# Low parts of weights by an adding DMA, expert picks by head, 40 U blocks ahead: a decoder block on one NeuronCore

## The chip, the cores and the metric

One core of one Trainium2 chip runs the whole program. The metric is the device time of one execution in microseconds (us). Times are taken from one launch; a run of the kernel before gave 1881.7 us as the median of three.

## What is computed

The reference is one decoder layer on 512 tokens of width 1024, in float32. A normed input goes through one projection `w_in`, whose 42 column blocks of 128 feed a gated causal depthwise convolution of 31 taps (GLU value and gate), 16 query heads and 2 key/value heads of windowed attention with sinks, and two sigmoid gates. The convolution branch is layer-normed, passed through silu and `w_conv_out`; the attention branch through `w_attn_o`; the gates merge them, `w_out` and a residual follow. The second half is a retrieval of experts, where every token picks 16 of 16384 experts in each of 8 heads:

```python
q = (h @ w_pq).reshape(B, S, PEER_HEADS, 2, PEER_DHALF)
sc = jnp.einsum("bshcd,hcnd->bshcn", q, sub_keys)
s_top, i_top = lax.top_k(sc, 16)
cand = s_top[..., 0, :, None] + s_top[..., 1, None, :]
best, pos = lax.top_k(cand, 16)
a = gelu(einsum("ced,cd->ce", u_emb[idx], hx))
out = einsum("ce,ced->cd", softmax(best) * a, v_emb[idx])
```

## The kernel before, in words

Every weight matrix is used as two float32r parts so that products keep float32's precision: `load_w` (lines 116 to 123) loads a block of 128x1024 by a DMA on SP's queue (`wraw`), ScalarE (ACT) rounds it into `whi` (line 120), and VectorE (DVE) subtracts to get `wlo` (line 122). `products` (125 to 132) then issues, for each of 8 slices k, three matmuls: high by high, high by low, low by high (lines 130, 131, 132). There are 346 such loads: 42 of `w_in`, 8 of `w_ao`, 8 of `w_co`, 16 of `w_out`, 16 of `w_pq`, 128 of `put` (the U rows of the experts, transposed) and 128 of `pv` (the V rows). Buffers: 4 for `wraw` (WRAW), 3 each for `whi` and `wlo` (WHL).

The stages in the order of the program:

- Norm and transposes; then the 42 blocks of `w_in`. `conv` (265) issues taps of the convolution on DVE, 7 after each block; `attend` (324) handles one of 16 attention units, with DVE for mask, maximum and the scaling by `den` (357), and ACT for the exponentials (348). `gate_block` (372) puts a sigmoid (374) straight after each of the 16 gate blocks. `glu` clears a strip of 30 columns on GpSimd (POOL, 292).
- Layer norm of the convolution (402 to 426), while `w_ao` runs; `w_co`; then `w_out` (444 to 464), where each load feeds 12 matmuls of 512 columns, three per accumulator and slice.
- Scores: 16 blocks of `w_pq`, each with a product by the sub-keys (498) and 4 top-16 searches on DVE (`top16`, 480); after each pair `head` (502) combines candidates.
- `choose` (514), once for each of the 4 chunks of 128 tokens, works out which expert and which gate (wide compares on 128x1024 at 539 to 542 and some 20 small ones). Chunk 0 is handled row by row; chunks 1 to 3 are "dense". For those `build_g` (563) builds a table of gates by expert: 24 groups of 16 tokens, each with one-hot factors `yt` and `xt` on DVE (584, 587; 8 tokens at a time, XT, two buffers each), 16 matmuls (592), four evictions on ACT (594) and a write of 1 MB to DRAM (`gd`, 595).
- U blocks: `u_step` (635) is a load of `put`, 24 matmuls of 384 columns and a gelu into `ga` (640). AHEAD = 31 of them are issued before the V stage, 4 before `choose`, one after each group of the build, the rest at the end; `ga` has AHEAD + 1 buffers.
- V stage (706 to 720): 128 steps. Each issues one further U block while there are any, a load of `pv`, the gates times `ga` split into `wh` and `wl` (653, 657, 658) and 18 matmuls of 512 columns (664 to 666); once in 8 steps it loads the gate table `gl` (648). Beside it run the 256 gathers of chunk 0 on POOL's queue (600), each with one instruction on DVE (615 or 623), paced by `due`. The residual rows `last` are loaded in the first three steps and added at the end.

The order on each engine is not the program's alone: instructions are placed ahead of time by a scheduler that lets later work through when earlier work isn't ready, so the first gelu of a U block stands at 638.3 us, before the last head's searches. On the chip each engine then keeps that order.

## Time and profile before

| | us |
|---|---|
| median of 3 runs (1878.46 to 1885.8) | 1881.7 |
| the profiled execution | 1897.27 |
| its span, first to last instruction | 1895.5 |

The profiled execution's granted TensorE clock is 0.959 of full speed on average. The profile gives for each engine its busy time, for each group of instructions of one line its busy time, the mean of one and what ended the idle time before it, and the chain of work that ended last. PE is TensorE, PEld its weight loads, SP the engine that issues most DMAs. Durations of matmuls overlap, so the distance from start to start is what a matmul costs.

### The profile page before, as it was taken

The numbers are of one execution on the slowest core, as the hardware profiler recorded it, in microseconds if no ns is written. First come the engines' busy times: TensorE is split into PE (matmuls) and PEld (weight loads), VectorE is DVE, ScalarE is ACT, GpSimd is POOL, SyncE is SP. The second block draws the span as 40 slices with busy tenths as digits, with TensorE's granted clock in tenths as the row PEclk, the third lists the DMA queues.
The fourth block names the chain that finished last, engine by engine and source line by source line (L and its number), as shares of the span: only waits on it lengthen the run. The fifth ranks groups of instructions, "written<-read, shape, count | busy, mean of one in ns | idle before, by whom it ended". The sixth has DMA issues, their size and how long they took to land.

```text
span 1895.5 us, 24387 instructions
## 1 busy us (share of the span) xinstructions
PE 1749.9 (92%) x8892; PEld 1535.2 (81%) x8892; DVE 1487.4 (78%) x2765; ACT 743.8 (39%) x1083; POOL 339.3 (18%) x268
## 2 busy tenths in 40 slices
PE   6998886999999999967599999999999999999997
PEld 5876664788787899957589989898988988998776
DVE  6998799585689999998577766775767776776787
ACT  5236543643522245546333333333333333333333
POOL 0000000000000000010043332432433432433341
PEclk9999886899999999988899999999999999999999
DMA  5332110133632234544689878887878887987884
GB/s 187 118 122 67 56 46 22 52 104 124 224 109 87 93 122 170 186 157 198 210 301 325 300 264 288 292 290 271 298 252 300 317 284 250 328 295 260 294 304 158
DMA packets 148776, 385.05 MB, mean 203 GB/s; under 512 B 12208, under 2 KB 63920, under 8 KB 145584
## 3 DMA queue, kind: packets, MB, share of 16 engines
q1 hardware_dynamic: 111792, 249.26, 38.3%
q0 software_dynamic: 36864, 134.23, 19.7%
q8 instruction: 70, 1.15, 0.2%
q14 instruction: 50, 0.41, 0.1%
HBM read 350.67 MB, written 29.88 MB: 201 GB/s over the span
## 4 chain that ended last, share of the span: by engine, by line
PE 65%; DVE 15%; DMA 8%; ACT 2%; issue 1%; SPq 0%; DVEq 0%; ACTq 0%
PE mm L130 12%; PE mm L132 12%; PE mm L131 12%; DMA gl<-gd 7%; PE tr L665 2%; PE tr L666 2%; PE sc L665 2%; PE ot L665 2%; PE sc L666 2%; PE tr L664 2%; PE ot L664 2%; PE ot L666 2%; PE sc L664 2%; DVE wlo L122 2%; DVE gl L653 2%; DVE yt L584 2%
## 5 line engine op out<-in xcount | busy, mean ns | idle before, releaser
L120 ACT ACTIVATE whi<-wraw 128x1024 fp32r<-128x1024 f32 x346 | 365.0, 1056 | 620.3 <-PE mm L131 550.4
L122 DVE TENSOR_TENSOR wlo<-wraw,whi 128x1024 fp32r<-128x1024 f32 x346 | 422.1, 1220 | 135.2 <-ACT whi L120 123.6
L132 PE MATMUL mm<-tTh,wlo 128*128 128x384 f32 (+2 forms) x1168 | 402.2, 344 | 14.5 <-DVE wlo L122 14.5
L130 PE MATMUL mm<-tTh,whi 128*128 128x384 f32 (+2 forms) x1168 | 401.2, 344 | 2.5 <-DVE x L459 1.4
L131 PE MATMUL mm<-tTl,whi 128*128 128x384 f32 (+2 forms) x1168 | 400.3, 343 | 0.2 <-DVE tTl L175 0.2
L600 POOL DMA_INDIRECT row<-pu,eidx x128 | 169.3, 1323 | 948.7 <-ACT gst L594 577.6
L132 PEld LDWEIGHTS mm<-tTh,wlo 128*128 128x128 f32 x1168 | 222.6, 191 | 22.6 <-DVE wlo L122 18.1
L130 PEld LDWEIGHTS mm<-tTh,whi 128*128 128x128 f32 x1168 | 222.7, 191 | 11.8 <-ACT whi L120 3.0
L131 PEld LDWEIGHTS mm<-tTl,whi 128*128 128x128 f32 x1168 | 222.4, 190 | 8.2 <-DVE tTl L175 0.4
L600 POOL DMA_INDIRECT row<-pv,eidx x128 | 169.0, 1320 | 311.1 <-DVE acc L623 283.0
L657 ACT ACTIVATE wh<-gl 128x384 fp32r<-128x384 f32 x128 | 67.3, 526 | 337.0 <-PE ot L665 316.4
L276 DVE SCALAR_TENSOR_TENSOR yconv<-uc,pc,yconv 128x512 f32<-128x512 f32 x240 | 169.3, 743 | 0.2
L623 DVE SCALAR_TENSOR_TENSOR acc<-row,gate,acc 128x1024 f32<-128x1024 f32 x128 | 164.2, 1283 | 6.2 <-DMA acc<-x2d 4.1
L130 PE MATMUL mm<-hTh,whi 128*128 128x512 f32 (+1 forms) x352 | 143.3, 408 | 22.9 <-ACT sgc L374 15.3
L615 DVE SCALAR_TENSOR_TENSOR row<-row,hrow 128x1024 f32<-128x1024 f32 x128 | 155.4, 1220 | 9.8 <-DMA row<-pu,eidx 9.6
L653 DVE TENSOR_TENSOR gl<-gl,ga 128x384 f32<-128x384 f32 x128 | 61.7, 553 | 107.1 <-DMA gl<-gd 90.8
L131 PE MATMUL mm<-hTl,whi 128*128 128x512 f32 (+1 forms) x352 | 140.3, 399 | 0.0
L132 PE MATMUL mm<-hTh,wlo 128*128 128x512 f32 (+1 forms) x352 | 139.5, 397 | 0.0
L658 DVE TENSOR_TENSOR wl<-gl,wh 128x384 fp32r<-128x384 f32 x128 | 71.1, 556 | 71.4 <-ACT wh L657 64.6
L664 PE MATMUL tr<-whi,wh 128*128 128x512 f32 x256 | 98.1, 392 | 15.3 <-ACT wh L657 15.3
L665 PE MATMUL tr<-wlo,wh 128*128 128x512 f32 x256 | 100.8, 396 | 3.3 <-DVE wlo L122 3.3
L130 PEld LDWEIGHTS mm<-hTh,whi 128*128 128x128 f32 x352 | 70.2, 200 | 41.3 <-ACT sgc L374 17.7
(248 smaller groups left out, 2957.5 us busy)
## 6 DMA issues: line engine op xcount, KB each, us to landing
wraw<-put SPq DMA_DIRECT2D x128, 512.0 KB, 4.2
wraw<-pv SPq DMA_DIRECT2D x128, 512.0 KB, 4.9
gd<-gst SPq DMA_DIRECT2D x24, 1024.0 KB, 7.3
gl<-gd SPq DMA_DIRECT2D x16, 1536.0 KB, 11.9
wraw<-w_in SPq DMA_DIRECT2D x42, 512.0 KB, 3.6
wraw<-w_out SPq DMA_DIRECT2D x16, 512.0 KB, 3.2
wraw<-w_pq SPq DMA_DIRECT2D x16, 512.0 KB, 4.1
wraw<-w_ao SPq DMA_DIRECT2D x8, 512.0 KB, 3.2
```

The lines of the kernel that those rows point to most:

```text
L120: nc.scalar.activation(hi, raw, AF.Copy)
L122: nc.vector.tensor_tensor(lo, raw, hi.bitcast(F32), op=OP.subtract)
L130: nc.tensor.matmul(p, wh[:, ks], xh[:, k], start=(k == 0), stop=False)
L131: nc.tensor.matmul(p, wh[:, ks], xl[:, k], start=False, stop=False)
L132: pace[0] = nc.tensor.matmul(p, wl[:, ks], xh[:, k], start=False, stop=(k == KB - 1))
L276: nc.vector.scalar_tensor_tensor(y[:, j], uc[:, t:t + S], w, y[:, j], op0=OP.mult, op1=OP.add)
L600: ins = nc.gpsimd.indirect_dma_start(out=r, out_offset=None, in_=table, in_offset=bass.IndirectOffsetOnAxis(ap=eidx[:, b, s:s + 1], axis=0))
L615: nc.vector.scalar_tensor_tensor(r, r, 1.0, h, op0=OP.mult, op1=OP.mult, accum_out=dots[:, s:s + 1])
L623: nc.vector.scalar_tensor_tensor(acc, r, gate[:, b, s:s + 1], acc, op0=OP.mult, op1=OP.add)
L664: nc.tensor.matmul(p, w[0][:, chunk(n)], v[0][:, ns], start=(i == 0), stop=False)
L665: nc.tensor.matmul(p, w[0][:, chunk(n)], v[1][:, ns], start=False, stop=False)
L666: pace[0] = nc.tensor.matmul(p, w[1][:, chunk(n)], v[0][:, ns], start=False, stop=(i == P - 1))
```

## The change

`load_w` has a second way, used from the second block of `w_in` after the first pair to the last U block ahead of the V stage (40 + 32 + 16 + 40 = 128 loads): ACT writes the negated high part into `wlo`, and an adding DMA on POOL's queue adds the block, read from DRAM a second time, onto it. DVE's subtraction stays for the first pair of `w_in` and for everything in the V stage. `products` and `w_out` put the matmuls on the low part last. There are 3 raw buffers and 4 each for the two parts. The scaling by `den` goes to ACT, the small clearing to DVE. The gate blocks are written with their bias only, and 16 sigmoids follow after the last tap. `choose` is split: `pick` runs once for each head on all four chunks (8 times, inside the heads' stage), `keys` once for each dense chunk. After each head 4 U blocks are issued (32), 8 more spread over the 24 groups: 40 ahead. The build takes 4 tokens at a time. The gate table is one tensor per chunk, loaded by three DMAs. `last` is loaded near the end into the buffers of the gathers, after these are drained.

```diff
-AHEAD = 31
+AHEAD = 40
+U_HEAD = 4
-U0 = 4
-XT = 8
+XT = 4
 WARM2 = 0
-GL_PARTS = 1
 GL_AT = 4
-WRAW = 4
-WHL = 3
+WRAW = 3
+WHL = 4
 GLU1 = 4
 GLU_U = 16
-G_U = 1
...
-    gd = dram.tile([P, NU // GT, P, GT], F32, name="gd")
+    NG = P // GT
+    gv = {}
+    for b in BUILT:
+        gv[b] = dram.tile([P, NG, P, GT], F32, name=f"gb{b}")
...
+    by_dma = [False]
+
     def load_w(src):
         raw = wp.tile([P, D], F32, name="wraw", bufs=WRAW)
         nc.sync.dma_start(raw, src)
         hi = wp.tile([P, D], F32R, name="whi", bufs=WHL)
         nc.scalar.activation(hi, raw, AF.Copy)
         lo = wp.tile([P, D], F32R, name="wlo", bufs=WHL)
-        nc.vector.tensor_tensor(lo, raw, hi.bitcast(F32), op=OP.subtract)
+        if by_dma[0]:
+            nc.scalar.activation(lo, hi.bitcast(F32), AF.Copy, scale=-1.0)
+            nc.gpsimd.dma_start(lo, src, accum_op=OP.add)
+        else:
+            nc.vector.tensor_tensor(lo, raw, hi.bitcast(F32), op=OP.subtract)
         return hi, lo
...
             ks = slice(k * P, (k + 1) * P)
             nc.tensor.matmul(p, wh[:, ks], xh[:, k], start=(k == 0), stop=False)
             nc.tensor.matmul(p, wh[:, ks], xl[:, k], start=False, stop=False)
+        for k in range(KB):
+            ks = slice(k * P, (k + 1) * P)
             pace[0] = nc.tensor.matmul(p, wl[:, ks], xh[:, k], start=False, stop=(k == KB - 1))
...
             conv(KB * TAPS, j - UC)
         if j == 0:
             ps0 = halves([a["w_in"][J_GATE], a["w_in"][J_VAL]], hT)
+            by_dma[0] = True
...
-        nc.gpsimd.memset(uc[:, :HALO], 0.0)
+        nc.vector.memset(uc[:, :HALO], 0.0)
         nc.vector.scalar_tensor_tensor(uc[:, HALO:], pv, bias(J_VAL + j), sg, op0=OP.add, op1=OP.mult)
...
-                nc.vector.tensor_scalar(sc[:, h], sc[:, h], den[:, h:h + 1], None, op0=OP.mult)
+                nc.scalar.activation(sc[:, h], sc[:, h], AF.Identity, scale=den[:, h:h + 1])
...
-        nc.scalar.activation(dst[:, j], p, AF.Sigmoid, bias=bias(o + j))
+        nc.scalar.activation(dst[:, j], p, AF.Identity, bias=bias(o + j))
...
     conv(KB * TAPS)
+    for t in (sga, sgc):
+        for j in range(KB):
+            nc.scalar.activation(t[:, j], t[:, j], AF.Sigmoid)
...
                     nc.tensor.matmul(p, mT[0][:, k, cs], hi[:, ns], start=(k == 0), stop=False)
-                    nc.tensor.matmul(p, mT[0][:, k, cs], lo[:, ns], start=False, stop=False)
-                    nc.tensor.matmul(p, mT[1][:, k, cs], hi[:, ns], start=False, stop=(k == KB - 1))
+                    nc.tensor.matmul(p, mT[1][:, k, cs], hi[:, ns], start=False, stop=False)
+            for c in range(2):
+                for n in range(2):
+                    ns = slice(n * 512, (n + 1) * 512)
+                    nc.tensor.matmul(acc[2 * c + n], mT[0][:, k, chunk(b0 + c)], lo[:, ns], start=False,
+                                     stop=(k == KB - 1))
...
-    eidx = rp.tile([P, NB, SLOTS], U32, name="eidx")
+    eidx = rp.tile([P, len(ROW_CHUNKS), SLOTS], U32, name="eidx")
     gate = rp.tile([P, NB, SLOTS], F32, name="gate")
-    keyT = rp.tile([P, 3, NB, P], F32, name="keyT")
+    keyT = rp.tile([P, 3, len(BUILT), P], F32, name="keyT")
...
-    sv = rt.tile([P, NB, 16, TOPK], F32, name="sv")
-    si = rt.tile([P, NB, 16, TOPK], U32, name="si")
-    bv = rt.tile([P, NB, HEADS, TOPK], F32, name="bv")
-    bp = rt.tile([P, NB, HEADS, TOPK], U32, name="bp")
+    sel = rt.tile([P, 2, NB, HEADS, TOPK], F32, name="sel")
...
-    def scores(hc):
+    def scores(hc, sv, si):
...
-            top16(sv[:, b, hc], si[:, b, hc], p[:, chunk(b)], KEYS)
+            top16(sv[:, b, hc % 2], si[:, b, hc % 2], p[:, chunk(b)], KEYS)
 
     def head(h):
-        s1, s2 = sv[:, :, 2 * h], sv[:, :, 2 * h + 1]
-        cand = rt.tile([P, NB, CAND], F32, name="cand", bufs=2)
+        sv = rt.tile([P, NB, 2, TOPK], F32, name="sv", bufs=2)
+        si = rt.tile([P, NB, 2, TOPK], U32, name="si", bufs=2)
+        for c in range(2):
+            scores(2 * h + c, sv, si)
+        s1, s2 = sv[:, :, 0], sv[:, :, 1]
+        cand = rt.tile([P, NB, CAND], F32, name="cand")
...
+        bv = rt.tile([P, NB, TOPK], F32, name="bv", bufs=2)
+        bp = rt.tile([P, NB, TOPK], U32, name="bp", bufs=2)
         for b in range(NB):
-            top16(bv[:, b, h], bp[:, b, h], cand[:, b], CAND)
-
-    def choose(b):
-        sh = [P, HEADS, TOPK]
-        t = {n: rt.tile(sh, F32, name="c_" + n) for n in ("p", "q", "r", "t", "e", "i", "j")}
+            top16(bv[:, b], bp[:, b], cand[:, b], CAND)
+        pick(h, si, bv, bp)
+
+    def pick(h, si, bv, bp):
+        sh = [P, NB, TOPK]
+        hs = slice(h * TOPK, (h + 1) * TOPK)
+        t = {n: rt.tile(sh, F32, name="c_" + n) for n in ("p", "q", "r", "t", "i", "j")}
...
-        sif = rt.tile([P, HEADS, 2, TOPK], F32, name="sif")
-        nc.vector.tensor_copy(sif, si[:, b].rearrange("p (h c) k -> p h c k", c=2))
-        wide = [P, HEADS // 2, TOPK, TOPK]
-        sel = []
+        sif = rt.tile([P, NB, 2, TOPK], F32, name="sif")
+        nc.vector.tensor_copy(sif, si)
+        wide = [P, NB, TOPK, TOPK]
         for s, src in ((0, t["i"]), (1, t["j"])):
-            r = rt.tile(sh, F32, name=f"sel{s}")
-            for h0 in (0, HEADS // 2):
-                hs = slice(h0, h0 + HEADS // 2)
-                eq = rt.tile(wide, F32, name="eq")
...
-                nc.vector.tensor_reduce(r[:, hs], eq, axis=AX.X, op=OP.add)
-            sel.append(r)
-        stt(t["e"], sel[0], float(KEYS), sel[1], op0=OP.mult, op1=OP.add)
-        nc.vector.tensor_copy(eidx[:, b], t["e"].rearrange("p h k -> p (h k)"))
-        gt = gate[:, b].rearrange("p (h k) -> p h k", h=HEADS)
-        tt(gt, bv[:, b], bv[:, b, :, 0:1].to_broadcast(sh), op=OP.subtract)
+            eq = rt.tile(wide, F32, name="eq")
+            tt(eq, src[:, :, :, None].to_broadcast(wide), iota[:, None, None, :TOPK].to_broadcast(wide),
+               op=OP.is_equal)
+            tt(eq, eq, sif[:, :, s, None, :].to_broadcast(wide), op=OP.mult)
+            nc.vector.tensor_reduce(sel[:, s, :, h], eq, axis=AX.X, op=OP.add)
+        for n, b in enumerate(ROW_CHUNKS):
+            stt(eidx[:, n, hs], sel[:, 0, b, h], float(KEYS), sel[:, 1, b, h], op0=OP.mult, op1=OP.add)
+        gt = gate[:, :, hs]
+        tt(gt, bv, bv[:, :, 0:1].to_broadcast(sh), op=OP.subtract)
         nc.scalar.activation(gt, gt, AF.Exp)
-        sm = small.tile([P, HEADS], F32, name="sm")
+        sm = small.tile([P, NB], F32, name="sm")
         nc.vector.tensor_reduce(sm, gt, axis=AX.X, op=OP.add)
         nc.vector.reciprocal(sm, sm)
         tt(gt, gt, sm[:, :, None].to_broadcast(sh), op=OP.mult)
...
-        if b in DENSE:
-            nc.vector.tensor_copy(u, sel[0])
-            ts(u, u, 4, None, op0=OP.logical_shift_right)
-            nc.vector.tensor_copy(t["p"], u)
-            stt(t["q"], t["p"], -float(LOW), sel[0], op0=OP.mult, op1=OP.add)
-            p = psum("tr")
-            for s, k in enumerate((t["p"], t["q"], sel[1])):
-                nc.tensor.transpose(p[:, chunk(s)], k.rearrange("p h k -> p (h k)"), ident)
-            nc.scalar.activation(keyT[:, :, b], p[:, :3 * P].rearrange("p (s t) -> p s t", s=3), AF.Copy)
+
+    def keys(b):
+        n = BUILT.index(b)
+        sh = [P, HEADS, TOPK]
+        hi, lo = (rt.tile(sh, F32, name="k_" + x) for x in ("p", "q"))
+        u = rt.tile(sh, U32, name="k_u")
+        s0 = sel[:, 0, b]
+        nc.vector.tensor_copy(u, s0)
+        nc.vector.tensor_scalar(u, u, 4, None, op0=OP.logical_shift_right)
+        nc.vector.tensor_copy(hi, u)
+        nc.vector.scalar_tensor_tensor(lo, hi, -float(LOW), s0, op0=OP.mult, op1=OP.add)
+        p = psum("tr")
+        for s, k in enumerate((hi, lo, sel[:, 1, b])):
+            nc.tensor.transpose(p[:, chunk(s)], k.rearrange("p h k -> p (h k)"), ident)
+        nc.scalar.activation(keyT[:, :, n], p[:, :3 * P].rearrange("p (s t) -> p s t", s=3), AF.Copy)
...
-            nc.sync.dma_start(gd[:, n * (P // GT) + g], st)
+            nc.sync.dma_start(gv[b][:, g], st)
...
-            step = NU // GT // GL_PARTS
-            for k in range(0, NU // GT, step):
-                nc.sync.dma_start(gl[i // GI][:, k:k + step], gd[:, k:k + step, i:i + GI, :])
+            for n, b in enumerate(DENSE):
+                nc.sync.dma_start(gl[i // GI][:, n * NG:(n + 1) * NG], gv[b][:, :, i:i + GI, :])
...
             for i, (v, w) in ops:
                 v_products(i, n, v, w)
 
-    for hc in range(16):
-        scores(hc)
-        if hc % 2:
-            head(hc // 2)
     ups = iter(range(P))
             if i is not None:
                 u_step(i)
 
-    up(U0)
-    left = AHEAD - U0
-    for b in DENSE:
-        choose(b)
+    for h in range(HEADS):
+        head(h)
+        up(U_HEAD)
+    left, groups = AHEAD - HEADS * U_HEAD, len(BUILT) * (P // GT)
+    done = 0
+    for b in BUILT:
+        keys(b)
         for _ in build_g(b):
-            if left and G_U:
+            done += 1
+            while done * (AHEAD - HEADS * U_HEAD) > (AHEAD - HEADS * U_HEAD - left) * groups:
                 up(1)
                 left -= 1
-    for b in ROW_CHUNKS:
-        choose(b)
     up(left)
+    by_dma[0] = False
     gctx.close()
     vp = ctx.enter_context(tc.tile_pool(name="vp", bufs=1, reuse_waits="tile"))
     rows = ctx.enter_context(tc.tile_pool(name="rows", bufs=1, reuse_waits="tile"))
     rowgen = by_rows()
     total, due = 2.0 * P - AHEAD, 0.0
     load_gates(0)
-    last = []
+    last = {}
     for i in range(P):
         up(1)
-        if i < ND:
-            nc.sync.dma_start(last[i], x2d[DENSE[i]])
         if i % GI == GL_AT:
         if i < P - 2:
             v_steps(i)
         elif i == P - 2:
+            for _ in rowgen:
+                pass
+            for n, b in enumerate(DENSE):
+                last[n] = rows.tile([P, D], F32, name="row", bufs=ROWS)
+                nc.sync.dma_start(last[n], x2d[b])
...
-    for _ in rowgen:
-        pass
```

## Rows read from the trace of the kernel before

**Rows 1.** the page, share and count of each engine, then the chain that ended last

```profile
PE 1749.9 (92%) x8892; PEld 1535.2 (81%) x8892; DVE 1487.4 (78%) x2765; ACT 743.8 (39%) x1083; POOL 339.3 (18%) x268
...
PE 65%; DVE 15%; DMA 8%; ACT 2%; issue 1%; SPq 0%; DVEq 0%; ACTq 0%
```

**Rows 2.** stretches: start:end, length, busy PE, PEld, DVE, ACT, POOL (count), clock, DMA share, GB/s

```profile
20.00:150.00 130.00, 125.68 (x620) 104.07 (x618) 121.34 (x200) 48.84 (x73) 0.25 (x2) 1.00 0.38 118
150.00:345.00 195.00, 159.84 (x731) 119.98 (x732) 175.94 (x348) 95.97 (x212) 0.37 (x3) 0.80 0.13 44
345.00:515.00 170.00, 170.00 (x785) 138.13 (x784) 106.70 (x158) 77.09 (x102) 0.00 (x0) 1.00 0.39 131
470.00:515.00 45.00, 45.00 (x203) 36.70 (x203) 28.72 (x41) 23.20 (x28) 0.00 (x0) 1.00 0.60 203
515.00:680.00 165.00, 155.32 (x849) 139.03 (x848) 155.42 (x867) 53.42 (x73) 0.00 (x0) 0.99 0.32 105
680.00:805.00 125.00, 124.03 (x815) 123.37 (x814) 122.20 (x161) 64.96 (x84) 0.00 (x0) 1.00 0.47 165
805.00:913.00 108.00, 73.25 (x519) 69.83 (x517) 94.93 (x104) 62.39 (x65) 6.12 (x4) 0.87 0.45 176
920.00:930.00 10.00, 2.56 (x6) 2.08 (x7) 3.73 (x8) 1.70 (x4) 0.00 (x0) 0.50 0.99 346
927.00:1747.00 820.00, 805.11 (x3993) 729.34 (x3994) 584.07 (x746) 278.19 (x384) 286.15 (x218) 0.98 0.82 287
1747.00:1882.00 135.00, 128.89 (x560) 105.57 (x560) 105.34 (x122) 47.38 (x65) 45.98 (x34) 0.99 0.75 265
```

**Rows 3.** the tile ga, 515 to 926 us: ns min/median/max, first and last start

```profile
L640 ACT ACTIVATE ga<-mm x32: 470/470/529, 638.3 to 796.4; 128x384 f32<-128x384 f32 x32
```

**Rows 4.** timeline of PE: first matmul of a U block, then of its V block

```profile
1200.45 0.33 PE L130 MATMUL mm<-tTh,whi 128*128 128x384 f32 x1
...
1204.64 0.39 PE L664 MATMUL tr<-whi,wh 128*128 128x512 f32 x1
```

**Rows 5.** stretches: length, DVE busy with line 122 alone (count), clock, DMA share, GB/s

```profile
20.00:150.00 130.00, 26.72 (x23) 1.00 0.38 118
150.00:345.00 195.00, 19.19 (x16) 0.80 0.13 44
515.00:680.00 165.00, 32.99 (x28) 0.99 0.32 105
```

**Rows 6.** groups on DVE, 0 to 375 us: busy us, mean ns of one, idle before

```profile
L357 DVE TENSOR_SCALAR sc<-sc,att_den 128x256 f32<-128x256 f32 (+1 forms) x64 | 17.2, 330 | 0.0
```

**Rows 7.** the page, costliest groups

```profile
L120 ACT ACTIVATE whi<-wraw 128x1024 fp32r<-128x1024 f32 x346 | 365.0, 1056 | 620.3 <-PE mm L131 550.4
L600 POOL DMA_INDIRECT row<-pu,eidx x128 | 169.3, 1323 | 948.7 <-ACT gst L594 577.6
```

**Rows 8.** groups of instructions on ACT, 0 to 375 us

```profile
L348 ACT ACTIVATE sc<-sc,att_nm 128x256 f32<-128x256 f32 (+1 forms) x64 | 30.1, 471 | 26.2 <-DVE att_nm L344 26.1
L374 ACT ACT_TABLE_LOAD x10 | 12.8, 1283 | 0.2
L374 ACT ACTIVATE sgc<-mm,pc 128x512 f32<-128x512 f32 x8 | 5.5, 690 | 0.1
```

**Rows 9.** groups of instructions on DVE, 515 to 925 us

```profile
L541 DVE TENSOR_TENSOR eq<-eq,sif 128x1024 f32<-128x1024 f32 x16 | 19.5, 1220 | 0.0
L576 DVE TENSOR_TENSOR xb<-keyT,iota 128x512 f32<-128x512 f32 x12 | 8.2, 685 | 0.0
L526 DVE TENSOR_TENSOR c_i<-c_i,c_t 128x128 f32<-128x128 f32 x4 | 1.1, 286 | 0.0
```

**Rows 10.** groups of instructions on PE, 515 to 925 us

```profile
L498 PE MATMUL sc<-sk,pq 128*128 128x128 f32 x128 | 18.2, 287 | 6.9 <-DVE topw L484 6.8
```

**Rows 11.** timeline of PE: eight matmuls of the table build

```profile
783.74 1.05 PE L592 MATMUL sc<-xt,yt 128*128 128x128 f32 x8
```

**Rows 12.** groups of instructions on ACT, 515 to 925 us

```profile
L594 ACT ACTIVATE gst<-ot 128x512 f32<-128x512 f32 x48 | 52.2, 1087 | 3.0 <-PE ot L592 2.9
```

More of the change, by code (lines that the diff above doesn't have):

```diff
@@ L35 @@
 DENSE = tuple(b for b in range(NB) if b not in ROW_CHUNKS)
+BUILT = DENSE
 ND = len(DENSE)
@@ L257, in rope_tables @@
             else:
-                nc.vector.tensor_scalar(dst, p, sign, None, op0=OP.mult)
+                nc.vector.tensor_scalar(dst, p, sign[:, 0:1], None, op0=OP.mult)
     y = None
@@ L575, in build_g @@
                 for t, w, k in ((xa, high, 0), (xb, LOW, 1)):
[L576 removed]
+                    nc.vector.tensor_tensor(t, keyT[:, k, n, cs, None].to_broadcast([P, XS, w]),
                                             iota[:, None, :w].to_broadcast([P, XS, w]), op=OP.is_equal)
@@ L583, in build_g @@
                 yt = gp.tile([P, XT, P], F32, name="yt", bufs=XB)
-                nc.vector.tensor_tensor(yt, keyT[:, 2, b, c, None].to_broadcast([P, XT, P]),
+                nc.vector.tensor_tensor(yt, keyT[:, 2, n, c, None].to_broadcast([P, XT, P]),
                                         iota[:, None, :].to_broadcast([P, XT, P]), op=OP.is_equal)
@@ L601, in gathered @@
             out=r, out_offset=None, in_=table,
-            in_offset=bass.IndirectOffsetOnAxis(ap=eidx[:, b, s:s + 1], axis=0))
+            in_offset=bass.IndirectOffsetOnAxis(ap=eidx[:, ROW_CHUNKS.index(b), s:s + 1], axis=0))
         tc.add_manual_dep(ins.ins, pace[0].ins.name,
@@ L704, in body @@
     load_gates(0)
-    last = []
+    last = {}
     for i in range(P):
         up(1)
-        if i < ND:
-            last.append(rows.tile([P, D], F32, name="last", bufs=ND))
-            nc.sync.dma_start(last[i], x2d[DENSE[i]])
         if i % GI == GL_AT:
```

12 lines of the change are left out of this document (4 added, 8 removed).

## The prediction

> **What bounds the kernel now.** I read the page first: PE is busy for 92% of the span and holds 65% of the chain that ended last, DVE 15%, DMA 8% [rows 1]. A busy PE isn't a PE at its peak, so I cut the span into stages, the second view, and compared three columns: PE, DVE and the count of matmuls [rows 2]. The reader is to see four regimes.
>
> - 150 to 345 us, attention and convolution: DVE is busy for 175.9 of 195 us, and PE places only 731 matmuls at a mean granted clock of 0.80 of 2.4 GHz, against 785 in 170 us at full clock behind it. DVE is the bound. From 20 to 150 us both are full (PE 125.7 and DVE 121.3 of 130).
> - 345 to 515 us, the three projections: PE is busy without a break. 170 us over 785 matmuls is 0.217 us each, so 5.2 us for a load with 24 matmuls and 2.6 us for one of `w_out` with 12.
> - 515 to 913 us, scores, choice of experts, build: DVE is full (155.4 of 165, then 122.2 of 125). PE keeps up only while it has U blocks. Their 32 gelus start between 638 and 796 us [rows 3], and from 805 to 913 us PE is busy for 73.3 of 108 us, as the build alone can't feed it.
> - From 927 us, the V stage: PE is busy for 805 of 820 us, with the DMA engines at a share of 0.82. A U block takes 4.19 us of PE (from its first matmul to the V block's first [rows 4]); one step with both takes 820 / 96 = 8.5 us, and the V blocks that are left without a U block take 135 / 31 = 4.35 us each.
>
> So DVE's work before 913 us costs time, and every U block done there instead of later saves a share of the V stage.
>
> **The terms.** The profiled execution took 1897.3 us, 15.6 over the median, and the sum is made against it; I carry the difference over to the median. About 0.5% (9 us) can be told from no change.
>
> *A. 20 to 345 us.* Removed from DVE: line 122 is 26.7 and 19.2 us here [rows 5], of which the first pair (2.4) stays, so 43.5 us; and the scaling by `den`, 17.2 us [rows 6]. DVE's 297 us fall to 236. The 8 small clearings that DVE gets have no row; they lie between nothing and the 0.29 us of an instruction on 128 columns [rows 9], at most 2.3 us, and I count them at nothing, in DVE's new slack. Added to ACT: 16 negations of 1.06 us in the second stretch, the length of line 120 with the same shape [rows 7], so 17 us; the scalings, 64 by 0.47 as the exponentials of that shape [rows 8], so 30 us; taken from it, the 10 table loads of the gate sigmoids, 13 us [rows 8]. ACT goes from 96 to about 130 of 195 us, DVE from 176 to between 115 and 140 (the lower where taps move up into the first stretch). PE's 731 matmuls would take 158 us at the 0.217 of the next stretch, and their weight loads are 120 us [rows 2]. Each attention unit is a chain through all three engines, and in the first stretch PE is full and gives nothing. Bounds: 0, if the chain is what takes the time, and -75 (195 to 120). I take **-35**, PE at the pace of the next stretch (195 to 160), since PE is then the fullest.
>
> *B. 345 to 515 us.* 36 subtractions leave DVE, worth nothing, since PE covers them. The adding DMAs may cost. For `w_out` a load has 2.6 us of PE. The 45 us of that stretch carry 203 GB/s, 9.1 MB; sixteen adding reads of 0.52 MB make 17.5 MB. The most that a 10 us stretch shows is 346 GB/s at a DMA share of 0.99 [rows 2]: 51 us, +6. If the engines spend a second pass on the part that lies in SBUF, 26 MB and 75 us, +30. ACT gets 17 us more here and would be busy for 40 of 45. I take **+12**, nearer the lower end, because four pairs of buffers can be filled during `w_co`. The 16 late sigmoids are 16 by 0.69 = 11 us of ACT [rows 8], between the last tap and the first product with a gate. ACT is busy for 77 of 170 us and PE has `w_ao` to do: 0, and +12 if that cover is gone. The sigmoids also stand on ACT's queue ahead of the layer norm, whose next user is `w_co`.
>
> *C. 515 to 927 us (412 us).* One head now holds on PE two loads of 5.2, 18.2 / 8 = 2.3 of sub-key products [rows 10] and four U blocks of 4.19: 29.5 us. On DVE it holds the searches, (155.4 - 33.0) / 8 = 15.3 [rows 2, 5], and `pick`: six wide instructions of 1.22 and about 18 small ones, 0.29 at twice their size [rows 9], taken as 0.25: 11.8, in all 27. Eight heads are 236 us, PE the bound by a little. On ACT 12 copies of 1.06, four gelus of 0.47 [rows 3] and two table loads of 1.28 between exponential and gelu are 17 us. The build: 24 groups, each with 8 instructions of 0.685 [rows 9] and about one more for the shared factors on DVE, 6.2 us; PE has four times up to 1.05 [rows 11], ACT four evictions of 1.09 [rows 12], 4.4. So 105 (ACT) to 149 us (DVE), taken as 140, nearest to DVE's, as the fullest engine. With 5 us to start, 12 for the last head's searches and the 14 us from the last write to the first V matmul that stand there now, the sum is 407: **-5**. Moved past SP's queue: nine loads of `put` and as many adding DMAs on POOL, which has nothing else until the gathers start; one gather keeps POOL for 1.32 us [rows 7], a third of a U block. On POOL an adding DMA waits for ACT's negation with only the next adding DMA behind it, and PE, which waits for the result, asks for it last, after 16 of its 24 matmuls. Bounds: -22, if U blocks and build fill PE together (370 us of matmuls plus the same ends), and +38, if the 8 U blocks in the build (34 us) hold up DVE, whose two factor buffers now cover 8 tokens instead of 16, and the groups take 6.2.
>
> *D. From 927 us.* Nine steps lose their U block: 9 x (8.5 - 4.35) = **-37**. If bytes bound the stage, nine loads of 0.52 MB at 287 GB/s are only -16. With three raw buffers and four pairs instead of four and three the count is the same; ACT stood waiting for PE to free a `whi` for 550 of its 620 us before line 120 [rows 7], so raw blocks lie ready and the fourth isn't missed; if they didn't, a step would see the load's latency. The three smaller loads of `gl` and the later `last` move off the 14 us in front of the stage, at most -6.
>
> The sum is -35 + 12 - 5 - 37 = -65: 1832 in the profile, **1817** as a median.
>
> The Trainium skill ("DMA: Bandwidth & Descriptors", section "Anatomy of one DMA") puts a DMA issued from GpSimd at about 2.0 us plus its bytes over 436 GB/s. An estimate from that is 3.2 us for an adding block, of which 1.2 are transfer; two such transfers fit into a `w_out` load, term B would be 0 and the sum 1805. No row of this trace shows an adding DMA, so the bounds from the rows stand.
>
> **Rivals.**
>
> *1. The adding DMA is slow, and weights come at its pace (slower).* A plain block at 346 GB/s holds the engines for 1.5 us. If an adding one holds them for 4.5 (read, read, write one after the other), a load costs 6.0. Heads: 36 instead of 29.5, +52; `w_ao` and `w_co`: 16 by 0.8, +13; `w_out`: 96 against 57, +39. -65 + 104 = +39, **1921**. It decides from 4.0 us on, where the extras are 28 + 5 + 31 and eat the gain. For it: six loads in a head and their adding twins leave only 3.4 us for one of these, and the V stage already shows share 0.82 with two queues at work. Against it: 20 to 345 us runs at shares of 0.38 and 0.13, and the scores at 0.32. Chance 0.18. The Trainium skill (same page, "Issuing engines are not separate DMA queues") says that DMAs of all issuers run on the same 16 engines; by that rule, POOL's queue adds no bandwidth, and the share of 0.82 agrees.
>
> *2. The relief isn't turned into time.* DVE gets free, but attention is bound by its chain, longer by ACT's scalings, and U blocks on PE stall the finer build: A -15, B +12, C +20, D -28, in sum -11, **1871**. For it: ACT and PE keep a fixed order, and 35 us of PE already go idle in the build; against it: DVE is at 90% and over where it matters. Chance 0.20. Here the change wouldn't do what it says.
>
> *3. Everything fills.* A -75, B +6, C -22, D -38: -129, **1753**. For it: no engine's floor forbids it; against it: PE never reached such filling beside attention. Chance 0.15.
>
> **How the numbers follow.** The forecast, 1780 to 1855, has 0.47. Range 1745 to 1895: rival 2 and most of rival 3 lie inside; about 0.13 of rival 1 is left out above, some 0.06 below. Faster by over 0.5%: 0.47 + 0.15 + 0.12 of rival 2 = 0.74. Within: 0.08 of rival 2 and 0.02 of rival 1, 0.10. Slower: 0.16.
>
> **What would show it.** Right: subtractions on DVE fall from 346 to 218; the last tap comes some 35 us earlier; PE has no waits on `wlo` in the heads; the last U block ahead ends within the build; the V stage keeps 8.5 and 4.35 us a step. Wrong: PE waiting for the adding DMA in the heads or `w_out` (rival 1), ACT nearly full with PE's clock still down between 150 and 345 us (rival 2), or a build over 6.5 us a group.

## The result, and the profile after

The changed kernel takes 1837.94 us (median of four runs, 1836.21 to 1839.78), the kernel before, timed beside it, 1883.75 (four runs, 1878.46 to 1893.36): a ratio of **0.9751, 95% interval 0.971 to 0.9793**, so 46 us faster. The profiled execution after took 1836.21 us with a span of 1834.4, close to its own median. The profiled execution before (1897.27) lies 13.5 us over the median of its four runs; that comes up again below.

The page of the kernel after, its counterpart to [rows 1]: share and count of each engine, the chain that ended last by engine, then by line.

```profile
PE 1734.7 (95%) x8892; PEld 1519.7 (83%) x8892; DVE 1346.5 (73%) x2741; ACT 918.5 (50%) x1297; POOL 463.9 (25%) x388
...
PE 85%; DMA 5%; DVE 5%; issue 3%; ACT 1%; SPq 0%; POOL 0%; DVEq 0%; POOLq 0%; ACTq 0%
PE mm L138 17%; PE mm L139 17%; PE mm L142 17%; PE sc L616 4%; PE tr L689 3%; PE tr L687 3%; PE tr L688 3%; PE sc L688 3%; PE sc L687 3%; PE sc L689 3%; PE ot L687 3%; PE ot L689 3%; PE ot L688 3%; DMA gl<-gb 2%; DMA wlo<-w_out 1%
```

PE's part of the chain went from 65% to 85%, DVE's from 15% to 5%. DVE lost 141 us of work (1487.4 to 1346.5), ACT gained 175 (743.8 to 918.5), POOL 125. The last entry of the chain is what the change brought in on the other side: the adding DMA of `w_out`, waited for. The gate table's load, the entry before it, stood for more in the chain of the kernel before:

```profile
PE mm L130 12%; PE mm L132 12%; PE mm L131 12%; DMA gl<-gd 7%; PE tr L665 2%; PE tr L666 2%; PE sc L665 2%; PE ot L665 2%; PE sc L666 2%; PE tr L664 2%; PE ot L664 2%; PE ot L666 2%; PE sc L664 2%; DVE wlo L122 2%; DVE gl L653 2%; DVE yt L584 2%
```

The stretches of the kernel after, cut at its own stages (columns as in [rows 2]):

```profile
20.00:150.00 130.00, 130.00 (x633) 108.64 (x633) 116.42 (x206) 71.29 (x97) 20.09 (x23) 1.00 0.91 218
150.00:322.00 172.00, 167.54 (x911) 127.96 (x910) 130.32 (x265) 151.01 (x331) 17.28 (x20) 0.96 0.54 121
322.00:412.00 90.00, 90.00 (x389) 72.89 (x388) 48.00 (x74) 53.13 (x61) 13.86 (x16) 1.00 0.87 212
412.00:478.00 66.00, 55.10 (x221) 42.06 (x220) 14.06 (x34) 42.67 (x51) 14.72 (x17) 0.91 1.02 271
478.00:740.00 262.00, 260.71 (x1477) 246.34 (x1476) 201.96 (x1013) 160.83 (x192) 46.35 (x53) 1.00 0.95 225
740.00:785.00 45.00, 43.67 (x304) 42.99 (x303) 33.31 (x50) 26.28 (x32) 0.00 (x0) 1.00 0.55 193
785.00:905.00 120.00, 89.31 (x600) 79.26 (x600) 104.28 (x175) 79.23 (x77) 3.52 (x3) 0.93 0.45 184
918.00:1635.00 717.00, 717.00 (x3608) 651.70 (x3609) 534.78 (x694) 257.39 (x348) 277.63 (x205) 1.00 0.85 301
1635.00:1822.00 187.00, 174.18 (x735) 142.37 (x734) 141.68 (x165) 59.78 (x82) 70.29 (x47) 0.95 0.77 270
```

In the order of the rows: the first 150 us fill PE (130 of 130), beside a DMA share that went from 0.38 to 0.91. Attention and convolution (second row) fill PE for 167.5 of 172 us at a granted clock of 0.96, where [rows 2] have 159.8 of 195 at 0.80. The projections after it (third row) fill PE as before. `w_out` (fourth row) is the one stretch where PE has holes beside a DMA share of 1. The heads (fifth) fill PE almost completely. In the build PE is full while the last U blocks run beside it (sixth) and at 89 of 120 behind them (seventh), with DVE at 104. The V stage (eighth) has PE at 717.0 of 717.0, and its steps without a U block (ninth) 174 of 187.

The milestones, by the tiles that the matmuls and evictions use (ns min/median/max, then first and last start). Before: the products of `w_co`, the products that read the normed second input (from the heads to the last U block), and the V products.

```profile
L130 PE MATMUL mm<-yTh,whi x64: 389/389/393, 426.5 to 469.4; 128*128 128x512 f32 x64
...
L130 PE MATMUL mm<-tTh,whi x1168: 281/334/667, 517.9 to 1745.8; 128*128 128x384 f32 x171, 128*128 128x512 f32 x18, 128*128 128x256 f32 x6
...
L664 PE MATMUL tr<-whi,wh x256: 387/389/795, 927.4 to 1880.4; 128*128 128x512 f32 x128
```

After, the same with the table's evictions between (before they ran from 718.2 to 911.2 us):

```profile
L138 PE MATMUL mm<-yTh,whi x64: 389/389/393, 368.5 to 409.7; 128*128 128x512 f32 x64
...
L138 PE MATMUL mm<-tTh,whi x1168: 278/334/422, 475.7 to 1632.9; 128*128 128x384 f32 x168, 128*128 128x512 f32 x21, 128*128 128x256 f32 x6
...
L618 ACT ACTIVATE gst<-sc x96: 1023/1060/1149, 735.9 to 904.1; 128x512 f32<-128x512 f32 x96
...
L687 PE MATMUL tr<-whi,wh x256: 387/389/796, 917.8 to 1816.7; 128*128 128x512 f32 x128
```

From these starts the time divides as follows, by the terms of the prediction. A is the time to the first product of `w_co`, B from there to the heads, C from the heads to the first V product, D to the last V product.

| term | before | after | difference | forecast |
|---|---|---|---|---|
| A | 426.5 | 368.5 | -58 | -35 |
| B | 91.4 | 107.2 | +16 | +12 |
| C | 409.5 | 442.1 | +33 | -5 |
| D | 953.0 | 898.9 | -54 | -37 |
| to the end of the span | 15.1 | 17.7 | +3 | 0 |
| sum | 1895.5 | 1834.4 | -61 | -65 |

### The profile page after: what moved, and what is told of

It reads as the page before. It is cut to its first block, busy times and chain, and to the rows that moved or that the text cites. A ratio compares the mean times of both kernels' runs of the same rounds, so it can differ in the third digit from the quotient of the medians.

```text
span 1834.4 us, 25060 instructions
## 1 busy us (share of the span) xinstructions
PE 1734.7 (95%) x8892; PEld 1519.7 (83%) x8892; DVE 1346.5 (73%) x2741; ACT 918.5 (50%) x1297; POOL 463.9 (25%) x388
## 4 chain that ended last, share of the span: by engine, by line
PE 85%; DMA 5%; DVE 5%; issue 3%; ACT 1%; SPq 0%; POOL 0%; DVEq 0%; POOLq 0%; ACTq 0%
PE mm L138 17%; PE mm L139 17%; PE mm L142 17%; PE sc L616 4%; PE tr L689 3%; PE tr L687 3%; PE tr L688 3%; PE sc L688 3%; PE sc L687 3%; PE sc L689 3%; PE ot L687 3%; PE ot L689 3%; PE ot L688 3%; DMA gl<-gb 2%; DMA wlo<-w_out 1%
## 5 line engine op out<-in xcount | busy, mean ns | idle before, releaser
L138 PE MATMUL mm<-tTh,whi 128*128 128x384 f32 (+2 forms) x1168 | 396.1, 340 | 1.5 <-DVE x L477 1.4
L130 DVE TENSOR_TENSOR wlo<-wraw,whi 128x1024 fp32r<-128x1024 f32 x218 | 265.9, 1221 | 44.3 <-ACT whi L124 40.1
L624 POOL DMA_INDIRECT row<-pv,eidx x128 | 179.8, 1405 | 271.0 <-DVE acc L647 246.6
L142 PE MATMUL mm<-tTh,wlo 128*128 128x384 f32 (+2 forms) x1168 | 235.0, 340 | 0.0
L142 PEld LDWEIGHTS mm<-tTh,wlo 128*128 128x128 f32 x1168 | 204.3, 188 | 3.8
L127 ACT ACTIVATE wlo<-whi 128x1024 fp32r<-128x1024 f32 x128 | 134.9, 1055 | 16.6 <-PE mm L142 12.2
L138 PE MATMUL mm<-hTh,whi 128*128 128x512 f32 (+1 forms) x352 | 137.0, 392 | 3.5 <-ACT hTh L184 2.6
L616 PE MATMUL sc<-xt,yt 128*128 128x128 f32 x768 | 110.3, 296 | 31.1 <-DVE xt L611 28.4
L616 PEld LDWEIGHTS sc<-xt,yt 128*128 128x128 f32 x768 | 99.6, 205 | 41.6 <-issue 22.1
L676 DVE TENSOR_TENSOR gl<-gl,ga 128x384 f32<-128x384 f32 x128 | 61.8, 553 | 90.7 <-DMA gl<-gb 90.7
L618 ACT ACTIVATE gst<-sc 128x512 f32<-128x512 f32 x96 | 99.3, 1064 | 53.5 <-PE sc L616 45.8
```

The lines of the kernel that those rows point to most:

```text
L130: nc.vector.tensor_tensor(lo, raw, hi.bitcast(F32), op=OP.subtract)
L138: nc.tensor.matmul(p, wh[:, ks], xh[:, k], start=(k == 0), stop=False)
L142: pace[0] = nc.tensor.matmul(p, wl[:, ks], xh[:, k], start=False, stop=(k == KB - 1))
L616: nc.tensor.matmul(p[:, t], yt[:, t1 + t], xt[:, t1 + t].rearrange("p a b -> p (a b)"), start=True, stop=True)
L624: ins = nc.gpsimd.indirect_dma_start(out=r, out_offset=None, in_=table, in_offset=bass.IndirectOffsetOnAxis(ap=eidx[:, ROW_CHUNKS.index(b) ...
```

## The experiments

All edits are to the changed kernel. Medians are of four runs, ratios against the kernel before on the same chip. Between profiles, a stage that an edit leaves alone agrees to 2 to 4 us (the stretch B, for one, lies between 105.5 and 107.4 in the six kernels that keep its code and buffers), so smaller differences of a stage tell nothing.

**Where the adding DMA is dear: `w_out` alone.** The subtraction on DVE is brought back for the 16 blocks of `w_out` only.

```diff
     tT = pair_x("tT")
+    by_dma[0] = False
     for b0 in range(0, NB, 2):
...
     fctx.close()
+    by_dma[0] = True
```

> The changed kernel, but the 16 blocks of w_out get their low parts from DVE again. Theory (an adding DMA holds the 16 DMA engines for two passes, and bounds w_out's stretch, 66 us at a DMA share of 1.02 against 45 before): the stretch falls back to about 45 us and the time to 1818 us. Rival (ACT's second copy or the residual and norm chain holds the stretch): it stays over 60 us and the time is 1833 us or more.

1822.63 us, ratio 0.9692 (0.9653 to 0.9731). `w_co` begins at 367.3 us and the heads at 458.8: 91.5 us between them, as before the change, against 107.2. So B's loss is the adding DMA and nothing else of the change. The waits of PE in the `w_out` stretch of the kernel after (total, times, longest):

```profile
PE mm L471 <- DMA wlo<-w_out: 4.0, 2, 2.4
PE sc L471 <- DMA wlo<-w_out: 3.3, 3, 2.4
PE ot L471 <- DMA wlo<-w_out: 2.2, 4, 0.8
```

and the same stretch without it, in the kernel with `w_out` on DVE:

```profile
408.00:459.00 51.00, 49.63 (x224) 40.23 (x223) 29.16 (x44) 29.34 (x35) 2.62 (x4) 1.00 0.67 214
```

With the adding DMA, line 471, the matmuls on the low part, waits for it in all three groups of accumulators, and the stretch runs at the DMA engines' pace: share 1.02 with 271 GB/s, 66 us for 16 blocks, so 4.1 us for a plain load and its adding twin. These waits are 9.5 us; the clock, 0.91 where it is 1.00 without them, makes up the rest. Without the adding DMA, share 0.67 and PE full. The theory (B's loss is the adding DMA) held.

**No adding DMA anywhere.**

```diff
-            by_dma[0] = True
+            by_dma[0] = False
```

> The changed kernel with DVE's subtraction for every block: no adding DMA at all. Theory (DVE's relief by the adding DMA is what paid): DVE gets 46 us back between 20 and 322 us and 6 x 1.1 us in each head, where it then needs 32 us against PE's 29.4; attention +25 to +40, heads +21, w_out -20, so 1865 to 1880 us. Rival (the gain came from the other parts, gates, buffers, order of the products, 9 more U blocks): 1838 us or less, about 1820 because w_out gets its 20 us back.

1850.83 us, ratio 0.9854 (0.9815 to 0.9893). The adding DMA as a whole is worth 13 us (12.9 by the spans of the two profiles). Stretches of this kernel, attention and the heads:

```profile
150.00:322.00 172.00, 144.01 (x772) 108.23 (x770) 164.98 (x303) 121.03 (x278) 0.00 (x0) 0.90 0.15 50
486.00:754.00 268.00, 266.71 (x1515) 252.33 (x1514) 256.80 (x1069) 114.26 (x146) 1.07 (x1) 1.00 0.37 118
```

and its milestones:

```profile
L138 PE MATMUL mm<-yTh,whi x64: 389/389/395, 394.2 to 435.5; 128*128 128x512 f32 x64
...
L138 PE MATMUL mm<-tTh,whi x1168: 278/334/423, 485.6 to 1648.6; 128*128 128x384 f32 x168, 128*128 128x512 f32 x21, 128*128 128x256 f32 x6
```

`w_co` starts 25.7 us later (394.2 against 368.5), with DVE at 165 of 172 us, PE at 144 and the clock at 0.90. From `w_co` to the heads 91.4 us, 16 fewer. In the heads DVE is back at 256.8 of 268, and they take 268.9 us up to the first eviction of the build against 260.2. PE is full in the heads of both kernels, and 3 of those 9 us come back in the build (165.1 us without adding, 168.2 with it). So the adding DMA gains 26 us in attention and some 6 in the heads and the build together, loses 16 in `w_out`, and the rest is within noise. The time lies between the theory's (1865 to 1880) and the rival's (1838 or less): the direction was as the theory had it, but the 21 us that it expected in the heads were too many. DVE has room there, just.

The two heads' rows also price an adding block. The kernel after has 0.95 x 262 = 249 us of DMA time and 225 GB/s x 262 = 59.0 MB; without adding it is 0.37 x 268 = 99 us and 118 x 268 = 31.6 MB. The plain blocks cost 99 / 60 = 1.6 us each (31.6 MB in blocks of 0.524), the 52 more cost 150 / 52 = **2.9 us** each.

**The adding taken from the DMA.** The second read stays, but overwrites.

```diff
-            nc.gpsimd.dma_start(lo, src, accum_op=OP.add)
+            nc.gpsimd.dma_start(lo, src)
```

> The changed kernel with POOL's second transfer made plain: the block is copied over the negated high part instead of added onto it, so the low parts are the full weights and the values are others; bytes from DRAM, queue and waits stay. Theory (the adding is what costs: two passes of the engines, 2.7 us a block, a plain one about 1.4): the stretch from the first w_co product to the first product of the heads falls from 107 us by 10 to 17, heads stay at 29.4 us each, about 1823 us. Rival (the second read from DRAM costs, adding is free): the stretch stays within 4 us, 1838 us.

1827.05 us, ratio 0.9729 (0.9706 to 0.9751). From `w_co` (368.7 us) to the heads (467.4) 98.7 us, 8.5 fewer, where the theory expected 10 to 17 and the rival at most 4: of B's 16, about half is the adding and half the second read. The division is rough, since the profiled execution (1830.0 us) is the longest of four from 1824.3 on. The queue's row on the page (packets, MB, share of the span), first of the kernel after:

```profile
q0 software_dynamic: 55296, 201.35, 41.8%
```

and without the adding, with its `w_out` stretch:

```profile
q0 software_dynamic: 55296, 201.35, 32.5%
```

```profile
410.00:467.00 57.00, 51.33 (x219) 41.24 (x217) 12.60 (x28) 41.04 (x46) 8.45 (x16) 0.94 0.93 322
```

The same bytes and packets take 0.418 x 1834.4 - 0.325 x 1828.2 = 173 us less over 128 blocks: adding costs 1.35 us of engine time a block, which agrees with 2.9 against 1.6. Here the engines move 322 GB/s at a share of 0.93, with adding 271 at 1.02.

**The gate sigmoids in their old place.**

```diff
-        nc.scalar.activation(dst[:, j], p, AF.Identity, bias=bias(o + j))
+        nc.scalar.activation(dst[:, j], p, AF.Sigmoid, bias=bias(o + j))
...
-    for t in (sga, sgc):
-        for j in range(KB):
-            nc.scalar.activation(t[:, j], t[:, j], AF.Sigmoid)
```

> The changed kernel with the sigmoid straight in each gate block again, and no late sigmoids. Theory (ACT is the fullest engine beside PE in the attention stretch, 151 of 172 us, so the table loads that come back, some 20 of 1.28 us, are partly exposed): +10 to +20 us, about 1852. Rival (ACT has slack there and the loads are hidden): within 4 us of 1838.

1836.75 us, ratio 0.978 (0.9738 to 0.9822): the same. The table loads on ACT up to 345 us say why. After (busy, mean ns, idle before):

```profile
L359 ACT ACT_TABLE_LOAD x10 | 12.8, 1283 | 0.2
L414 ACT ACT_TABLE_LOAD x9 | 11.5, 1283 | 0.2
L300 ACT ACT_TABLE_LOAD x2 | 2.6, 1283 | 0.0
```

with the sigmoids early:

```profile
L385 ACT ACT_TABLE_LOAD x9 | 11.5, 1283 | 0.2
L359 ACT ACT_TABLE_LOAD x8 | 10.3, 1283 | 0.1
L300 ACT ACT_TABLE_LOAD x2 | 2.6, 1283 | 0.0
L357 ACT ACT_TABLE_LOAD x2 | 2.6, 1283 | 0.0
```

21 loads in both. The late sigmoids (line 414) stand late in the program only; the scheduler lets them through as their gates come ready, between exponentials, and each such place costs a load again. The theory that ten loads are saved fell. ACT was even less busy with the early form (143.0 against 151.0 of 172 us), as 16 instructions are fewer, and the time is the same: ACT isn't the bound in attention.

**The scaling by `den` back on DVE.**

```diff
-                nc.scalar.activation(sc[:, h], sc[:, h], AF.Identity, scale=den[:, h:h + 1])
+                nc.vector.tensor_scalar(sc[:, h], sc[:, h], den[:, h:h + 1], None, op0=OP.mult)
```

> The changed kernel with the scaling by den on DVE again. Theory (ACT is now the fullest after PE in attention, 151 of 172 us against DVE's 130): ACT loses 30 us, DVE gains 17, the stretch gets shorter by 5 to 10 us, about 1830. Rival (DVE is still what holds attention, through the convolution): the stretch gets longer by 10 us or more, about 1850.

1853.94 us, ratio 0.9862 (0.9826 to 0.9898). Attention in this kernel:

```profile
150.00:322.00 172.00, 150.68 (x846) 116.28 (x846) 146.01 (x326) 127.36 (x263) 14.82 (x17) 0.93 0.47 104
```

`w_co` starts at 385.5 us, 17.0 later: just the 17.2 us of those 64 instructions [rows 6]. PE falls to 150.7 of 172 and the clock to 0.93. From 20 to 345 us PE now waits for 22.3 us in all, 12.8 of them for the scaled scores:

```profile
PE tr L370 <- DVE sc L368: 12.8, 2, 7.5
```

In the kernel after PE waits for 4.5 us there, and DVE stands idle before the layer norm's mean:

```profile
DVE yconv L422 <- ACT mu L419: 17.5, 1, 17.5
```

So with the scaling on DVE attention is paced by DVE again, though DVE is busy for only 146 of 172 us; with the scaling on ACT it is PE that is full, and DVE has slack. The theory that ACT has become the bound fell.

**32 U blocks ahead, then also 8 tokens at a time.** First `AHEAD`, then `XT` as well.

```diff
-AHEAD = 40
+AHEAD = 32
...
-XT = 4
+XT = 8
```

> The changed kernel with 32 U blocks ahead, all in the heads, none in the build. Theory (U blocks in the build are worth their 4.15 us in the V stage but hold up the build's two small buffers for about half of that): the V stage +33, the build -15, about 1855 us. Rival 1 (they are hidden in the build): +33, 1870 us. Rival 2 (they cost there what they save): 1838 us.

> As the run with 32 U blocks ahead, but the build takes 8 tokens at a time as before the change. Theory (the 4-token build is slower: more and shorter instructions on DVE and buffers that cover less): the build, from the first eviction to the last, is 10 to 20 us shorter than in that run, and so is the time. Rival (the group is bound by evictions and matmuls): no difference over 4 us.

1849.02 us (0.9852, 0.9833 to 0.987) and 1844.91 us (0.9827, 0.9809 to 0.9845). Milestones of the kernel with 32 ahead:

```profile
L618 ACT ACTIVATE gst<-sc x96: 1024/1058/1095, 736.8 to 890.9; 128x512 f32<-128x512 f32 x96
...
L687 PE MATMUL tr<-whi,wh x256: 387/389/794, 904.8 to 1831.6; 128*128 128x512 f32 x128
```

and with 32 ahead and 8 tokens:

```profile
L618 ACT ACTIVATE gst<-sc x48: 1024/1056/1094, 738.2 to 881.0; 128x512 f32<-128x512 f32 x48
...
L687 PE MATMUL tr<-whi,wh x256: 387/389/795, 900.1 to 1827.6; 128*128 128x512 f32 x128
```

The first came out as the theory had it: the 8 U blocks cost 14 us in the build (168.2 with them, 154.1 without) and bring 28 in the V stage (926.8 without, 898.9 with): worth having. The form with 4 tokens costs the build another 11 us (154.1 against 142.8; 96 evictions become 48), of which only 4 reach the end, also because the first V product then comes 19.1 us after the last eviction instead of 13.9. So the second theory held for the build, and not for the time.

**The buffers, the order of the low part, one gate table.** `WRAW`, `WHL` = 4, 3; the loops in `products` joined into one again; the three tables one tensor with one load.

```diff
-WRAW = 3
-WHL = 4
+WRAW = 4
+WHL = 3
```

> The changed kernel with 4 raw buffers and 3 of each part, as before the change. Theory (the adding DMA lengthens the life of a pair, so the fourth pair is what keeps PE fed in the heads and in w_out): heads over 29.4 us each, w_out longer, and the V stage, which fell by 12 us more than nine U blocks account for, longer by some of that: 1850 us or more. Rival (the count of pairs is covered): within 4 us of 1838.

```diff
-        for k in range(KB):
-            ks = slice(k * P, (k + 1) * P)
             pace[0] = nc.tensor.matmul(p, wl[:, ks], xh[:, k], start=False, stop=(k == KB - 1))
```

> The changed kernel with the matmuls on the low part between the others again in every block of 24 (w_out and the V products keep their order). Theory (in the V stage of the kernel before, PE stood 12 us inside U blocks waiting for DVE's low part, and the new order removes that): the V stage grows by about 12 us, and the stretches fed by the adding DMA by some more: 1850 us. Rival (four pairs of buffers cover the low part anyway): within 4 us of 1838.

```diff
-            for n, b in enumerate(DENSE):
-                nc.sync.dma_start(gl[i // GI][:, n * NG:(n + 1) * NG], gv[b][:, :, i:i + GI, :])
+            nc.sync.dma_start(gl[i // GI], gd[:, :, i:i + GI, :])
```

> The changed kernel with one gate table and one load of 1.5 MB in place of three of 0.5 MB. Theory (the three loads are part of what the V stage gained beyond the nine U blocks): the V stage is 5 to 10 us longer and the start of it 3 us later, about 1846 us. Rival (the same bytes at the same place): within 4 us of 1838.

1843.33 (0.9813, 0.9786 to 0.984), 1848.36 (0.9823, 0.9784 to 0.9862) and 1840.44 us (0.9785, 0.9749 to 0.9822). Each interval overlaps that of the change, so only the profiles tell more. Three pairs of parts cost 5 us between `w_co` and the heads (112.3 against 107.2) (with one buffer less for the parts, the adding DMA can run ahead by one block less; that this is how was not tested), and nothing in the heads or the V stage, where the theory had it too. The old order costs 12.7 us of span (1847.1 against 1834.4), but in small pieces: 5 before `w_co`, 2.5 in `w_out`, 2.5 in the build, 2.5 in the V stage, nothing in the heads; each of the 2.5 is within what profiles differ by. That it would lie in the V stage fell. With one table the V stage is 6 us longer in the profile (904.9 against 898.9), as its theory had it, but the medians lie 2.5 us apart: no difference that can be told.

**Two versions put together.** `w_out` on DVE as in the first experiment, with the gate table asked for three steps earlier; then with 8 tokens at a time and 37 ahead besides.

```diff
-GL_AT = 4
+GL_AT = 1
...
-XT = 4
+XT = 8
-AHEAD = 40
+AHEAD = 37
```

> The changed kernel with DVE's subtraction for w_out and the gate loads issued three steps earlier. Theory (w_out -17 as measured; the gate load takes 11 to 12 us, and in the steps without a U block three steps of 4.1 us more give it time, so DVE's and PE's waits for it there go): 1812 us. Rival (the loads only move in front of weight loads on SP's queue, which then come late): 1822 us, as with w_out alone.

> The same, with the build 8 tokens at a time and, to make room for its buffers, 37 U blocks ahead. Theory (8 tokens at a time make the build 11 us shorter; three U blocks less ahead cost the V stage 3 x 3.5 and save the build 3 x 1.8): 6 us under the run before it. Rival (the U blocks wait longer in front of the larger buffers' work and the gain is eaten): equal or up to 6 us more.

1822.49 us (0.9701, 0.9664 to 0.9737) and **1813.41 us (0.965, 0.9615 to 0.9685)**. The earlier table adds nothing to the 1822.63 of `w_out` alone, as the rival had it. In the steps without a U block DVE still waits for `gl`, for 28.8 us in 4 waits against 19.2 in 3 in the kernel after, and these steps stay at 4.7 us; the theory that the waits go fell. The milestones of the second:

```profile
L620 ACT ACTIVATE gst<-sc x48: 1026/1054/1112, 719.8 to 865.5; 128x512 f32<-128x512 f32 x48
...
L689 PE MATMUL tr<-whi,wh x256: 387/389/796, 885.4 to 1794.0; 128*128 128x512 f32 x128
```

Its build takes 145.7 us against 169.2 in the first, its V stage begins 15 us earlier, and the three U blocks fewer ahead give 7.5 of that back (908.6 us from the first to the last V product, 901.1 in the first). It is faster than both kernels.

## Why the prediction was right, and which of its terms were not

The forecast was 1817 us, "faster" by 65; it is 1838 and faster by 46. The mechanism held: DVE is relieved where it bounded, PE fills, and U blocks leave the V stage. Step by step:

*The sum against the profiled execution.* In the profiles the kernel lost 61 us of the 65 forecast. What turned 1832 into 1817 is the step "I carry the difference over to the median": before's profiled execution lay that far over its median, after's didn't (1836.21 against 1837.94). An offset of one execution isn't a property of the kernel, and carrying it over is 15 of the 21 us by which the number was off. That the 61 came so near the 65 is luck: A and D together gave 40 us more than forecast, B, C and the end 44 less.

*A, -35 forecast, -58 measured: right in kind, too small.* PE became the fullest engine, as the step chose: busy for 297.5 of the 302 us from 20 to 322, with DVE idle before the mean, which is there at 324.3 us instead of 376.2. What was too small is the pace. The "0.217 of the next stretch" is of products of 512 columns almost alone, while attention's matmuls are shorter: in their own stretch the kernel after places 911 matmuls in 172 us, 0.189 each. By an estimate from that, 731 take 138 us, 57 less than the 195. Part by part, 26 come from the adding DMA, 17 from `den` on ACT, 5 from the order, nothing from the gates; if they add up, some 10 are open. A step inside the term failed, "the 10 table loads of the gate sigmoids" taken off ACT: with the sigmoids late or early, 21 loads stand there. The kernel before had 30 on its lines (ten each at 374 and 348, six at 289, four at 346, up to 375 us), so nine did go, and which part of the change took them isn't shown. It cost nothing, as the early sigmoids showed.

*B, +12 forecast, +16 measured.* The term was right in kind and place: PE waits on `wlo` in `w_out`, and with DVE's subtraction there all of it goes. The value taken lay 4 us under what was measured, the bound with a second pass on the SBUF side (+30) 14 over it, and the bound by bytes (+6) 10 under it. The 0 taken for the 16 late sigmoids was right. The estimate from the Trainium skill ("DMA: Bandwidth & Descriptors", section "Anatomy of one DMA") put B at 0; the measurement, +16, decides: the bytes alone aren't the price of an adding block.

*C, -5 forecast, +33 measured: the term that failed.* The heads are as predicted. The exponential of each head's gates on ACT, in the timeline of the kernel after (start, length), marks their pace:

```profile
509.91 0.26 ACT L566 ACTIVATE gate<-gate 128x64 f32<-128x64 f32 x1
...
715.61 0.26 ACT L566 ACTIVATE gate<-gate 128x64 f32<-128x64 f32 x1
```

From one to the next it is (715.61 - 509.91) / 7 = 29.4 us, against 29.5 forecast, with PE at 260.7 of 262. What failed is "the build ... 105 (ACT) to 149 us (DVE), taken as 140": it took 168.2, 7.0 us a group. DVE in the last two thirds of the build, 785 to 905 us, groups by line:

```profile
L608 DVE TENSOR_TENSOR yt<-keyT,iota 128x512 f32<-128x512 f32 x74 | 51.0, 689 | 13.6 <-PE sc L616 10.9
L611 DVE TENSOR_TENSOR xt<-xa,xb 128x512 f32<-128x512 f32 x74 | 49.9, 685 | 0.0
L600 DVE TENSOR_TENSOR xb<-keyT,iota 128x512 f32<-128x512 f32 x9 | 6.2, 684 | 0.0
```

Four `yt` make a group, so these 120 us hold 18.5 groups, 6.5 us each. DVE has four of each of the two long lines a group, 5.5 us, and the shared factors, `xb` and two like it, on top: by their lengths the 6.2 of the step. They overlap a little (DVE is busy for 104 of the 120 us, 5.6 a group), and 0.7 a group go into waiting for PE (`sc`). The 5.5 groups before took 785 - 735.9 = 49 us, 8.9 each, while PE had the last U blocks between them. So the step's own upper end was about the price, DVE's 6.2 (154.1 us without U blocks between are 6.4 a group), and "if the 8 U blocks in the build hold up DVE" came true: 14 us, as 32 ahead showed. The other 14 of the 28 us over 140 are in large part the 4 tokens at a time: with 8 the build without U blocks took 142.8. That is rival 2's place and its sign ("a build over 6.5 us a group"), inside a case where its attention part did not come: the relief was turned into time there.

*D, -37 forecast, -54 measured.* The nine pairs fewer (a pair is a step with a U block) gave 9 x (8.525 - 4.34) = -38, as forecast. Beside that, pairs went from (1745.8 - 927.4) / 96 = 8.525 to (1632.9 - 917.8) / 87 = 8.22 us, -26, and steps without a U block from 4.34 to (1816.7 - 1632.9) / 40 = 4.60, +10. "The V stage keeps 8.5 and 4.35 us a step" was wrong in both. No single revert brings 8.5 back: 8.22 with 32 ahead, 8.21 with the old buffers, 8.23 with the old order, 8.21 with one table. The trace of the kernel before shows what went. From 927 to 1747 us PE waits inside U blocks for DVE's low part (total, times, longest):

```profile
PE mm L132 <- DVE wlo L122: 14.5, 9, 3.1
```

Eight of these waits come 4.5 to 5.5 us after DVE has stood waiting for the gate table, with the subtraction behind that on its queue; one such pair from the timelines of DVE and PE (start, length, what it waited for before):

```profile
1116.12 3.84 DVE L653 TENSOR_TENSOR gl<-gl,ga 128x384 f32<-128x384 f32 x8 [8.22 <-DMA gl<-gd]
...
1121.62 0.69 PE L132 MATMUL mm<-tTh,wlo 128*128 128x384 f32 x1 [3.13 <-DVE wlo L122]
```

From 1090 to 1140 us the granted clock is 0.93, from 1200 to 1300, without such a wait, 1.00. In the kernel after DVE waits for `gl` as long (90.7 us in the V stage, 90.8 before), but PE never for `wlo` from 918 to 1635 us, and the clock is 1.00. Over the 96 pairs before, the difference is 96 x (8.525 - 8.22) = 29 us: 14.5 of these waits and, for the rest, the clock, 0.98 over the 820 us against 1.00. With the old order alone, or the old buffers alone, the waits stay away too; that both together bring them back wasn't tried, and how much of it is peculiar to the execution before, 13.5 us over its median, is open.

Of the +10 in the steps without a U block, 5.8 stand in front of the last two V blocks (timelines of ACT and PE in the kernel after):

```profile
1808.21 1.06 ACT L173 ACTIVATE wraw<-acc 128x1024 f32<-128x1024 f32 x1 [1.82 <-DVE acc L647]
...
1811.87 1.22 PE L687 MATMUL tr<-whi,wh 128*128 128x512 f32 x2 [5.82 <-ACT whi L124]
```

The change drains the gathers before these two blocks, so the norm of chunk 0 (line 173) stands on ACT's queue ahead of their `whi`. The kernel before has no such wait; no run undoes this. Beside it the clock is lower, 0.95 in these steps against 0.99; how the rest divides is open.

*The rivals.* Rival 1, a slow adding DMA, was to decide "from 4.0 us on"; it measured 2.9, under the 3.4 that the rival left for it in the heads. PE never waited for it there, though at a DMA share of 0.95 little was to spare; only in `w_out`, with half the PE time per load, did it come out. By the Trainium skill (same page, "Issuing engines are not separate DMA queues") POOL's queue adds no bandwidth; the shares of 0.95 and 1.02, of both queues together, agree. Rival 3 fell with the build. Of the signs named, subtractions on DVE went from 346 to 218, PE had no waits on `wlo` in the heads, and the last U block ahead came within the build; the last tap starts 69 us earlier (279.0 against 347.6), not 35.
